# A row softmax: the first store is issued behind five instead of fourteen exponentials of the second tile

## The chip, the core and the metric

The kernel runs on one core of a Trainium2 chip. The engines that matter are VectorE (DVE), ScalarE (ACT), the sequencer SP that issues the loads, and the core's 16 DMA engines. The metric is the device time of one execution in microseconds, as the median of several runs.

## The reference

The input is 16 x 1024 x 512 float32 (33.55 MB), and the output has the same size. Every row of 512 gets a softmax at temperature 0.5:

```python
x_scaled = x / 0.5
x_max = np.max(x_scaled, axis=-1, keepdims=True)
exp_x = np.exp(x_scaled - x_max)
return exp_x / np.sum(exp_x, axis=-1, keepdims=True)
```

## The kernel before

The 16384 rows are cut into 8 tiles (c = 0 to 7). A tile has 128 partitions with 16 rows each, 4 MB, and a row's 512 elements lie one after another in its partition. Six buffers hold tiles; tiles 6 and 7 take the buffers of tiles 0 and 1, so their loads wait until the stores of those have landed. Everything is computed in place.

Tile 0 is loaded in two parts (4 rows and 12 rows of each partition), the others whole. All loads go through SP's queue (L66). All stores go through ACT's queue (L120), one for each tile, so ACT issues them in its own stream of instructions.

The work is cut into 11 blocks. Tile 0 has three (blocks 0, 1 and 2 with 4, 4 and 8 rows), tiles 1 to 6 are one block each (blocks 3 to 8), and tile 7 has two of 8 rows (blocks 9 and 10). A block goes through these steps:

- `shift` (L68): VectorE finds the negative maximum of each row (L74) and doubles it (L78): the bias. The load is issued here too, if the tile has none yet.
- `exponentials` (L80): ACT takes exp(2x + bias) row by row, one instruction for 512 elements of every partition, and sums as it goes (L86).
- `scale_vector` (L96): VectorE takes the reciprocals of the sums (L101) and multiplies the first rows, seven eighths of the block (L103).
- `scale_scalar` (L107): ACT multiplies the remaining rows, one for a block of 8 and two for a block of 16 (L112).
- `store` (L116): behind the tile's last block, the whole tile is written out.

The schedule is written by hand: each engine runs its instructions in the order of the program, and waits only where data or a buffer is missing. In step i of the loop ACT gets the exponentials of block i + 1, then the scaling of block i's last rows, then the store; VectorE gets the scaling of block i, then the maximum of block i + 2. `rows` (L127) cuts a block's exponentials into those ahead of the scaling and the store of the block before and those behind them. Only block 3, all of tile 1, is cut; the store beside it is that of tile 0, the first of the kernel.

Of the kernel before, what the change touches and what calls it, by code (L numbers as in the profile page):

```python
# [1 line left out]

# [4 lines left out]


@with_exitstack
def kernel(  # L10
    ctx: ExitStack,
    tc: tile.TileContext,
    x: bass.AP,
    out: bass.AP,
):
    nc = tc.nc
    fp32 = mybir.dt.float32
    P = nc.NUM_PARTITIONS
    AX = mybir.AxisListType.X
    EXP = mybir.ActivationFunctionType.Exp  # L20
    COPY = mybir.ActivationFunctionType.Copy
    MAX = mybir.AluOpType.max

    D = x.shape[-1]
    xf = x.flatten_outer_dims()
    of = out.flatten_outer_dims()
    N = xf.shape[0]

    G = 16
    C = N // (P * G)
    assert C * P * G == N
    xr = xf.rearrange("(c p g) d -> c p g d", p=P, g=G)
    outr = of.rearrange("(c p g) d -> c p g d", p=P, g=G)
    WHOLE = [(0, G)]
    LOADS = [[(0, 4), (4, G)]] + [WHOLE] * 7
    BLOCKS = [[(0, 4), (4, 8), (8, G)]] + [WHOLE] * 6 + [[(0, 8), (8, G)]]
    STORES = [WHOLE] * 8  # L40
    BMAX = 16
    BUFS = 6

    data = ctx.enter_context(tc.tile_pool(name="data", bufs=BUFS))
    stats = ctx.enter_context(tc.tile_pool(name="stats", bufs=6))

    ctx.enter_context(tc.manual_schedule())


    warm = stats.tile([P, 1], fp32, name="warm", bufs=1)  # L50
    nc.vector.memset(warm, 0.0)  # L51
    nc.scalar.activation(out=warm, in_=warm, func=EXP)  # L52

    chunks = {}
    blocks = [(c, lo, hi) for c in range(C) for lo, hi in BLOCKS[c]]
    n = len(blocks)
    biases, sums, recips = {}, {}, {}

    def load(c):
        if c < BUFS:  # L60
            chunks[c] = data.tile([P, G, D], fp32, name="xt")
        else:
            chunks[c] = chunks[c - BUFS]
        xt = chunks[c]
        for lo, hi in LOADS[c]:
            nc.sync.dma_start(out=xt[:, lo:hi, :], in_=xr[c][:, lo:hi, :])  # L66

    def shift(i):  # L68
        c, lo, hi = blocks[i]
        if c not in chunks:  # L70
            load(c)
        b = hi - lo
        negmax = stats.tile([P, BMAX], fp32, name="negmax")
        nc.vector.tensor_reduce(  # L74
            negmax[:, 0:b], chunks[c][:, lo:hi, :], axis=AX, op=MAX, negate=True
        )
        biases[i] = stats.tile([P, BMAX], fp32, name="bias")
        nc.vector.tensor_scalar_mul(biases[i][:, 0:b], negmax[:, 0:b], 2.0)  # L78

    def exponentials(i, rows):  # L80
        c, lo, hi = blocks[i]
        if i not in sums:
            sums[i] = stats.tile([P, BMAX], fp32, name="sums")
        for g in rows:
            row = chunks[c][:, lo + g, :]
            nc.scalar.activation(  # L86
                out=row,
                in_=row,
                func=EXP,
                bias=biases[i][:, g : g + 1],  # L90
                scale=2.0,
                accum_out=sums[i][:, g : g + 1],
            )


    def scale_vector(i):  # L96
        c, lo, hi = blocks[i]
        b = hi - lo
        k = b - b // 8
        recips[i] = stats.tile([P, BMAX], fp32, name="recip")  # L100
        nc.vector.reciprocal(recips[i][:, 0:b], sums[i][:, 0:b])  # L101
        rows = chunks[c][:, lo : lo + k, :]
        nc.vector.tensor_mul(  # L103
            rows, rows, recips[i][:, 0:k].unsqueeze(2).broadcast_to((P, k, D))
        )

    def scale_scalar(i):  # L107
        c, lo, hi = blocks[i]
        b = hi - lo
        for g in range(b - b // 8, b):  # L110
            row = chunks[c][:, lo + g, :]
            nc.scalar.activation(  # L112
                out=row, in_=row, func=COPY, scale=recips[i][:, g : g + 1]
            )

    def store(i):  # L116
        c, _, end = blocks[i]
        for lo, hi in STORES[c]:
            if hi == end:
                nc.scalar.dma_start(  # L120
                    out=outr[c][:, lo:hi, :], in_=chunks[c][:, lo:hi, :]
                )

    shift(0)
    shift(1)

    def rows(i):  # L127
        c, lo, hi = blocks[i]
        cut = hi - lo - (2 if c == 1 else 0)
        return range(cut), range(cut, hi - lo)  # L130

    exponentials(0, rows(0)[0])
    for i in range(n):
        if i + 1 < n:
            exponentials(i + 1, rows(i + 1)[0])
        scale_vector(i)
        scale_scalar(i)
        if i + 2 < n:
            shift(i + 2)
        store(i)  # L140
        if i + 1 < n:
            exponentials(i + 1, rows(i + 1)[1])


# [1 line left out]
_INS = ['x']  # L146
_OUTS = [((16, 1024, 512), 'float32')]


# [23 lines left out]
```

## Time and profile before

| what | us |
|---|---|
| median of 5 runs (162.05 to 162.61) | 162.33 |
| the profiled execution | 162.41 |
| its span, first to last instruction | 160.6 |
| VectorE busy | 134.6 |
| ACT busy | 102.2 |
| a maximum over 128x8192 (L74) | 8.68 |
| a scaling of 14 rows, 128x7168 (L103) | 7.62 |
| an exponential of one row (L86) | 0.71 |
| first store issued | 44.11 |
| last store issued | 147.50 |

Times inside an execution count from the span's start. In the profile's lines a group is named by line, engine, operation and what it writes and reads, `out<-in`; `xt` is a tile, `negmax`, `bias`, `sums` and `recip` are the small vectors of a block. `q1` and `q10` are the queues that the DMA engines serve, loads and stores. `ACTq` and `SPq` are instructions of the sequencers that issue DMAs; a DMA's issue takes under a microsecond, and its data moves later. "To landing" counts from the issue to the moment at which the whole transfer is announced.

### The profile page before, as it was taken

Reading aid. Unit: us, or ns where it says so; the run is one execution under the profiler, and the core shown is the slowest. Engines: PE = TensorE matmul, PEld = TensorE weight load, DVE = VectorE, ACT = ScalarE, POOL = GpSimd, SP = SyncE. Lnnn points to the kernel's source line nnn. Section 1 sums busy time; section 2 is a strip of 40 time slices with the busy share of each in tenths; the row PEclk is TensorE's granted clock in tenths of the full one; section 3 lists DMA queues with packets and bytes.
Section 4 is the critical chain, followed back from the end, with each engine's and each line's share of the span. In section 5 each row is a group of like instructions: output and inputs, shape, how many; then the busy total and the mean of one; then the engine's idle time right before and its main releaser. Section 6 shows DMA issues by size and latency. Waiting matters only on the chain.

```text
span 160.6 us, 402 instructions
## 1 busy us (share of the span) xinstructions
DVE 134.6 (84%) x45; ACT 102.2 (64%) x273; POOL 0.2 (0%) x4
## 2 busy tenths in 40 slices
DVE  0607999999999999999999999999999999957000
ACT  3071549069989963998199909990999890790000
POOL 0000000000000000000000000000000000000000
DMA  5999999999999999999999999999999999999993
GB/s 182 471 408 490 408 400 498 408 392 475 433 375 392 416 408 481 416 392 490 424 392 490 424 392 475 432 392 449 465 392 432 481 392 408 490 408 408 490 408 139
DMA packets 2450, 67.13 MB, mean 418 GB/s; under 512 B 272, under 2 KB 272, under 8 KB 272
## 3 DMA queue, kind: packets, MB, share of 16 engines
q1 hardware_dynamic: 1296, 33.56, 49.3%
q10 hardware_dynamic: 1152, 33.55, 48.4%
q14 instruction: 2, 0.02, 0.0%
HBM read 33.55 MB, written 33.55 MB: 418 GB/s over the span
## 4 chain that ended last, share of the span: by engine, by line
DVE 80%; DMA 7%; ACT 4%; issue 0%; SPq 0%
DVE negmax L74 42%; DVE xt L103 36%; DMA xt<-in_x_dram 7%; ACT xt L86 4%; DVE bias L78 1%; DVE recip L101 1%; SPq L66 0%
## 5 line engine op out<-in xcount | busy, mean ns | idle before, releaser
L86 ACT ACTIVATE xt<-xt,bias 128x512 f32<-128x512 f32 x128 | 90.4, 707 | 41.5 <-DVE bias L78 40.6
L74 DVE TENSOR_REDUCE negmax<-xt 128x16 f32<-128x8192 f32 (+2 forms) x11 | 69.9, 6353 | 9.5 <-DMA xt<-in_x_dram 9.5
L103 DVE TENSOR_TENSOR xt<-xt,recip 128x7168 f32<-128x7168 f32 (+2 forms) x11 | 62.0, 5637 | 0.4
L86 ACT ACTIVATION_READ_ACCUMULATOR xt<-xt,bias 128x1 f32 x128 | 23.8, 186 | 0.0
L112 ACT ACTIVATE xt<-xt,recip 128x512 f32<-128x512 f32 x15 | 9.9, 706 | 0.0
L101 DVE RECIPROCAL recip<-sums 128x16 f32<-128x16 f32 (+2 forms) x11 | 2.4, 219 | 1.8 <-ACT xt L86 1.8
L78 DVE TENSOR_SCALAR bias<-negmax 128x16 f32<-128x16 f32 (+2 forms) x11 | 1.9, 173 | 0.4
L52 ACT ACT_TABLE_LOAD x1 | 1.3, 1283 | 0.7 <-PEq L157 0.7
L51 DVE MEMSET warm<- 128x1 f32 x1 | 0.1, 59 | 0.8 <-PEq L157 0.8
L52 ACT ACTIVATE warm<-warm 128x1 f32<-128x1 f32 x1 | 0.2, 203 | 0.0
L157 POOL MEMSET const-bfloat16-1.0<- 128x1 bf16 x1 | 0.1, 101 | 0.0
L157 POOL MEMSET const-uint8-127<- 128x1 uint8 x1 | 0.1, 101 | 0.0
L157 POOL MEMSET const-float32-0.0<- 128x1 f32 x1 | 0.1, 98 | 0.2 <-issue 0.2
L157 POOL MEMSET const-float32-1.0<- 128x1 f32 x1 | 0.1, 98 | 0.0
## 6 DMA issues: line engine op xcount, KB each, us to landing
out_dram<-xt ACTq DMA_DIRECT2D x8, 4096.0 KB, 23.1
xt<-in_x_dram SPq DMA_DIRECT2D x7, 4096.0 KB, 30.1
xt<-in_x_dram SPq DMA_DIRECT2D x1, 3072.0 KB, 11.7
xt<-in_x_dram SPq DMA_DIRECT2D x1, 1024.0 KB, 4.8
```

The costliest lines, as they stand in the source:

```text
L51: nc.vector.memset(warm, 0.0)
L52: nc.scalar.activation(out=warm, in_=warm, func=EXP)
L74: nc.vector.tensor_reduce(negmax[:, 0:b], chunks[c][:, lo:hi, :], axis=AX, op=MAX, negate=True)
L78: nc.vector.tensor_scalar_mul(biases[i][:, 0:b], negmax[:, 0:b], 2.0)
L86: nc.scalar.activation(out=row, in_=row, func=EXP, bias=biases[i][:, g : g + 1], scale=2.0, accum_out=sums[i][:, g : g + 1],)
L101: nc.vector.reciprocal(recips[i][:, 0:b], sums[i][:, 0:b])
L103: nc.vector.tensor_mul(rows, rows, recips[i][:, 0:k].unsqueeze(2).broadcast_to((P, k, D)))
L112: nc.scalar.activation(out=row, in_=row, func=COPY, scale=recips[i][:, g : g + 1])
L157: nc = _bacc.Bacc("TRN2", target_bir_lowering=False, num_devices=1)
```

## The change

Block 3 is cut behind its fifth exponential instead of its fourteenth. ACT runs five exponentials of tile 1, scales the last row of tile 0, issues tile 0's store, and then runs the other eleven exponentials. Before it ran fourteen, scaled, stored, and ran two. Nothing else moves, on ACT or on any other engine.

```diff
     def rows(i):
         c, lo, hi = blocks[i]
-        cut = hi - lo - (2 if c == 1 else 0)
+        cut = 5 if c == 1 else hi - lo
         return range(cut), range(cut, hi - lo)
```

## The prediction

> **What bounds the kernel now.** I read the page's shares first, then the chain of work that ended last, then the DMA rows and queues.
>
> ```profile
> span 160.6 us, 402 instructions
> DVE 134.6 (84%) x45; ACT 102.2 (64%) x273; POOL 0.2 (0%) x4
> DMA  5999999999999999999999999999999999999993
> q1 hardware_dynamic: 1296, 33.56, 49.3%
> q10 hardware_dynamic: 1152, 33.55, 48.4%
> DVE 80%; DMA 7%; ACT 4%; issue 0%; SPq 0%
> ```
>
> Two resources are full. VectorE is named by the chain, but it stops at 147.4 us, 13.2 us before the end. The DMA engines are busy in every slice from the second to the last but one: q1 (loads) and q10 (stores) take 97.7% of the span, 156.9 us. The busy-time table of three stretches says what they move (columns: stretch, its length, DVE, ACT and POOL busy with counts, clock, DMA share, GB/s):
>
> ```profile
> 1.70:41.00 39.30, 30.43 (x15) 19.62 (x55) 0.00 (x0) 1.00 1.01 428
> 49.00:113.00 64.00, 63.73 (x17) 47.97 (x131) 0.00 (x0) 1.00 1.00 434
> 116.00:159.00 43.00, 29.46 (x11) 23.37 (x62) 0.00 (x0) 1.00 0.98 424
> ```
>
> Loads alone, loads beside stores, and stores alone run at one rate. So a store that comes earlier does not make the engines faster or slower; it takes turns from the loads. The size of a turn: q10's 1152 packets are 8 x 128 data packets of 32 KB and 8 x 16 tiny ones that announce the end, so 48.4% x 16 x 160.6 / 1024 = 1.21 us for a data packet on its engine; a 4 MB tile is 8 on each of 16 engines, 9.7 us alone.
>
> How turns are shared is read from the transfers' landings, each asked for by the stretch of its issue. Loads of tiles 1 and 2 (issued 1.62 and 2.09) land after 20.9 and 30.1 us, at 22.5 and 32.2: 9.7 apart, alone. Tiles 5, 6 and 7 land at 76.9, 96.2 and 116.3 (issued 3.82, 68.41, 87.79; 73.1, 27.8 and 28.5 later): 19.3 and 20.1 apart, beside stores. Loads and stores alternate one to one, and a load beside a store takes twice as long.
>
> The last load decides what follows. These are the landing times in the DMA answers for issues of 68 to 69 and of 87.5 to 88 us, the first store's, and the last store's:
>
> ```profile
> xt<-in_x_dram SPq DMA_DIRECT2D x1, 4096.0 KB, 27.8
> xt<-in_x_dram SPq DMA_DIRECT2D x1, 4096.0 KB, 28.5
> out_dram<-xt ACTq DMA_DIRECT2D x1, 4096.0 KB, 24.2
> out_dram<-xt ACTq DMA_DIRECT2D x1, 4096.0 KB, 12.3
> ```
>
> And these, from the timeline, are the instructions that they meet:
>
> ```profile
> 33.60 3.89 DVE L103 TENSOR_TENSOR xt<-xt,recip 128x3584 f32<-128x3584 f32 x1
> 37.03 0.71 ACT L86 ACTIVATE xt<-xt,bias 128x512 f32<-128x512 f32 x1
> 43.38 0.70 ACT L112 ACTIVATE xt<-xt,recip 128x512 f32<-128x512 f32 x1
> 44.11 0.38 ACTq L120 DMA_DIRECT2D out_dram<-xt  x1
> ...
> 103.88 8.68 DVE L74 TENSOR_REDUCE negmax<-xt 128x16 f32<-128x8192 f32 x1
> ...
> 120.50 4.41 DVE L74 TENSOR_REDUCE negmax<-xt 128x8 f32<-128x4096 f32 x1
> ...
> 147.50 0.34 ACTq L120 DMA_DIRECT2D out_dram<-xt  x1
> ```
>
> Tile 7 lands at 116.3 and VectorE asks for it at 120.50: a slack of 4.2 us, the number on which this change turns. Tile 6 lands at 96.2 and is asked for at 103.88, a slack of 7.7; tile 5 at 76.9 for 87.26, 10.4.
>
> **The change, part by part.** Nothing is added or removed. On ACT, nine of block 3's exponentials go from before the last-row scaling and the first store to behind them; the order on VectorE and SP is the same.
>
> *ACT and the moved issue.* The exponentials step by 0.705 us, so the sixth started at 37.03; there the last-row scaling now runs, to 37.74. It needs the reciprocal of 33.37, long there. The store also waits for VectorE's scaling of seven rows, which ends at 33.60 + 3.89 = 37.49. That is 0.25 us before ACT arrives, so the wait costs nothing; if VectorE were later by more, eleven instead of two exponentials of block 3 would stand behind the waiting store, and VectorE's reciprocal of their sums at 46.20 behind those. Today the last sum is ready at 45.87 + 0.19 = 46.06, 0.14 us ahead. The move leaves that: 16 exponentials, one scaling and one issue (a 0.45 us gap) in another order. The store goes out at 37.77 instead of 44.11, 6.34 us earlier. Cost on the path: 0, at most some tenths.
>
> *The loads.* Each store packet that comes earlier sits between load packets. 6.34 us of earlier start are 6.34 / 1.21 = 5.2 packets, so 5 or 6 on each engine, and all later loads land 5 x 1.21 = 6.1 us later (6 packets: 7.3). This holds only if the store queue never runs dry, which would give turns back. It does not: the first store would take from about 42.4 (issue + the 4.6 us between issue and first packet that the packet records show today) to about 61.8, and the second is issued at 58.97, the next ones at 75.59, 92.21 and 108.83, each before the one ahead is through at 19.4 us apiece (81, 100.6, 120). SP's queue is fed too: load 6 is let go when store 0 has landed, at about 62, and load 5 runs until about 82.
>
> *Who feels it.* Tile 5: 76.9 + 6.1 = 83.0, wanted at 87.26. Tile 6: 102.3, wanted at 103.88, still in time by 1.6. Tile 7: 116.3 + 6.1 = 122.4, wanted at 120.50: VectorE stands for 1.9 us. Here is the one uncertain size. The packet records put the ends of load 7 at 113.5 to 114.0 us on fifteen engines and at 115.85 on one, which lags by 1.87 us, or 1.5 packets. A lag of one packet only would give 1.25 us; no lag, 116.3 - 1.87 + 6.1 = 120.5 and a wait of nothing; a sixth packet, 3.1. Between 1.25 and 1.9 I take 1.55, since one engine out of sixteen is enough and the packets' order at the first store's entry makes one fall behind easily.
>
> *From VectorE to the end.* Behind the late reduce of L74 everything is serial: scaling of tile 6 (7.62), the second half's maximum (4.41), its scaling, eight exponentials on ACT, the last scaling, the last store. The one gap, 1.79 us before the reciprocal at 143.29, is spent waiting for ACT's exponentials, which hang on the same chain. So the last store goes out at 147.50 + 1.55 = 149.05. Meanwhile the engines will have done all other transfers at 148.5 to 149.7, as today, since they are full until then and tile 6's store (issued at 133.02 + 1.9 at most) is still ahead of its turn. What today's backlog costs the last store is small: it lands after 12.3 us, and on free engines 9.7 us plus what a small load shows beyond its bytes: 1 MB in 4.8 us, less 1.05 MB / 428 GB/s = 2.45, 2.35; together 12.05. So 0.25 us of the delay is absorbed. The sum: +1.55 - 0.25 = **+1.3 us**. The ends: 0 (no wait) and 3.1 - 0.25 = 2.9.
>
> The Trainium skill would price the last store differently: "DMA: Bandwidth & Descriptors", section "Anatomy of one DMA — SWDGE (gpsimd) path", fits 2.0 us plus bytes over 436 GB/s, 11.6 us for 4.19 MB, as an estimate. By that the backlog absorbs 0.7 us and the sum would be +0.85; the fit is for another issuing path, and the 4.8 us row is of this kernel.
>
> The profiled execution has 162.41 us, 1.8 more than its span; the median of five is 162.33. 162.33 + 1.3 = **163.6 us**.
>
> **The rivals.**
> - *No engine lags, and the load is just in time (same, 162.3).* By the working above the wait then is 0.0 to 0.2 us, which the 0.25 absorbs. For it: the lag of one engine grew out of small irregularities that need not come again. Against it: sixteen engines must all keep step.
> - *Faster, by the backlog.* If the earlier store meant less work left for the engines at 147.5, the last store would run on free ones: 147.50 + 12.05 instead of 12.3, -0.25, and with the 1.87 us lag of one engine gone as well at most some 0.9 us less: 161.5. It decides where tile 7 lands before 120.50 and the engines lose less when the first store enters: the stretch 41.0 to 48.7 us moves 400 GB/s against 428, a loss of 7.7 x 0.065 = 0.5 us. Against it: the engines are full, and order does not change the sum.
> - *The first store takes hold sooner (slower still).* If its 4.6 us shrink to about 1, as for the first load, which the packet records show moving 1.0 us after its issue, loads lose more turns. The limit is store 1's issue at 58.97: it then starts at about 60 instead of 68.1, so no more than 8.1 us are lost. Tile 7 lands at 124.4, the wait is 3.9 us, the time 162.33 + 3.65 = 166.0.
> - *The store's wait blocks ACT.* VectorE would have to be over 0.25 us later than it is at 37.49; each further us would go through the sums to 46.20. Nothing ahead of it changes, so this stays at some tenths.
>
> **How the numbers follow.** A measurement can tell about 0.2%, 0.33 us, from no change. The slower case with a wait of 1 to 2.2 us: 0.57 (own range 162.8 to 164.3). Just in time, and the blocked ACT with it: 0.27. Sooner hold or a sixth packet: 0.10. Faster: 0.06. The first and third are slower but for a small part: slower 0.69, same 0.25, faster 0.06. The range of 8 in 10 reaches into the just-in-time case below (162.1) and to a sixth packet above (2.9 less the last few tenths: 164.9).
>
> **What would show it.** The first store issued near 37.8 us with no wait; loads of tiles 4 to 7 landing about 6 us later; an idle time of 1 to 2 us on VectorE before the first 128x4096 maximum of tile 7, ended by the DMA; the last store's issue later by as much. If tile 7 lands by 120.5, the load's step was wrong; if VectorE waits and the end does not move, the backlog's.

## The result, and the profile after

The changed kernel takes 162.69 us (median of 25 runs, 162.39 to 164.62 and one of 166.64) against 162.22 us for the kernel before (46 runs, 162.03 to 162.61). The ratio is 1.0035 with a 95% interval of 1.0025 to 1.0045. Ratios leave out executions that took over 1.5% longer than the fastest of their kernel, here the one of 166.64 us. It is slower, as forecast, but by 0.47 us by the medians and not by 1.3, and its times spread further. The profiled execution took 162.48 us, near the lower end; that of the kernel before took 162.41, above its median. So these two profiles are only 0.07 us apart, and most of the 0.47 us is not in them.

The page of the changed kernel, to set beside the lines of the prediction:

```profile
span 160.7 us, 402 instructions
DVE 134.7 (84%) x45; ACT 102.2 (64%) x273; POOL 0.2 (0%) x4
DMA  5999999999799999999999999999999999999994
q1 hardware_dynamic: 1296, 33.56, 49.4%
q10 hardware_dynamic: 1152, 33.55, 48.6%
q14 instruction: 2, 0.02, 0.0%
DMA 46%; DVE 34%; ACT 11%; issue 1%; SPq 0%
```

The engines compute for the same time. The chain of work that ended last has moved from VectorE (80% before) to the DMA (46%): somewhere an engine now waits for a transfer. And the two DMA queues take 98.0% of 160.7 us where they took 97.7% of 160.6: 157.5 instead of 156.9 us for the same bytes.

The timeline of the changed kernel, with the same instructions as in the prediction:

```profile
37.19 0.71 ACT L112 ACTIVATE xt<-xt,recip 128x512 f32<-128x512 f32 x1
37.93 0.37 ACTq L120 DMA_DIRECT2D out_dram<-xt  x1
...
104.04 8.68 DVE L74 TENSOR_REDUCE negmax<-xt 128x16 f32<-128x8192 f32 x1
...
121.24 4.42 DVE L74 TENSOR_REDUCE negmax<-xt 128x8 f32<-128x4096 f32 x1 [0.49 <-DMA xt<-in_x_dram]
...
148.23 0.34 ACTq L120 DMA_DIRECT2D out_dram<-xt  x1
```

The first store goes out at 37.93, with no wait, as forecast. VectorE does wait for tile 7: 0.49 us of idle time ahead of the maximum at 121.24. The last store goes out at 148.23 instead of 147.50, 0.73 us later; 0.16 us of that is a later start of the whole program's work (104.04 against 103.88), and 0.57 is the wait with what hangs on it.

The landings of the loads of tiles 6 and 7 (issued 62.73 and 82.62), of the first store and of the last one, each from the answer for the stretch of its issue:

```profile
xt<-in_x_dram SPq DMA_DIRECT2D x1, 4096.0 KB, 39.1
xt<-in_x_dram SPq DMA_DIRECT2D x1, 4096.0 KB, 38.6
out_dram<-xt ACTq DMA_DIRECT2D x1, 4096.0 KB, 24.7
out_dram<-xt ACTq DMA_DIRECT2D x1, 4096.0 KB, 11.6
```

Tile 6 lands at 101.8, tile 7 at 121.2. It landed at 116.3 before, so the load lost 4.9 us, four turns of 1.21, and not five. This is the landing on the slowest engine. By the packet records its last packet of this load stood behind 27 store packets in the kernel before, where the other fifteen engines had 26; in the changed kernel it stands behind 31, and the others behind 30 or 31. The last store lands 11.6 us after its issue, where it took 12.3: 0.7 us of its delay is made up at once. Its last data end at 159.50 us, against 159.42 before.

One relation holds in all twenty profiles of this study and orders what follows: **the device time is the end of the last store's data plus 2.95 to 3.04 us.** The end of the data is that of the slowest of 16 DMA engines. In the kernel before fifteen of them end at 158.3 to 158.8 and one at 159.42; in the changed one they end at 158.8 to 159.5. The middle engine ends 0.65 us later, the last one 0.08. The records name no engine: packets are put together to sixteen chains in which one begins as the one before ends, so single counts of engines can be off by one or two.

### The profile page after: what moved, and what is told of

It is laid out like the page before. It is cut to its first block, busy times and chain, and to the rows that moved or that the text cites. A ratio compares the mean times of both kernels' runs of the same rounds, so it can differ in the third digit from the quotient of the medians.

```text
span 160.7 us, 402 instructions
## 1 busy us (share of the span) xinstructions
DVE 134.7 (84%) x45; ACT 102.2 (64%) x273; POOL 0.2 (0%) x4
## 4 chain that ended last, share of the span: by engine, by line
DMA 46%; DVE 34%; ACT 11%; issue 1%; SPq 0%
DMA xt<-in_x_dram 31%; DVE negmax L74 20%; DMA out_dram<-xt 15%; DVE xt L103 12%; ACT xt L86 10%; ACT xt L112 1%; DVE bias L78 1%; DVE recip L101 0%; SPq L66 0%
```

## The experiments

Kernels named "before with" or "changed with" differ from that kernel by the lines shown. Ratios are to runs of the kernel before on the same chip, with the 95% interval.

### The changed kernel once more

> The changed kernel once more, unaltered, for a second profile of it. Theory A (VectorE waits for tile 7's load; the wait varies from execution to execution because it is set by the DMA engine that lags most): ratio 1.002 to 1.005 to the kernel before, VectorE's wait before the first half's maximum of tile 7 anywhere from 0 to 2 us, and the last store's issue later than 147.5 by that wait. Theory B (the added time is lost on the DMA engines, where the packets of the two queues meet differently, and VectorE's wait is beside the point): the same ratio, but data of the last store ends later by more or less than VectorE's wait explains.

Measured: 1.0027 (1.0014 to 1.0040). In its profile VectorE idles 0.88 us ahead of tile 7's first half, the last store goes out at 148.40, the data end at 159.66. The wait is 0.4 us longer than in the first profile, the end 0.16 us later. That fits both theories, and left the question open.

### Taking the wait, or its consequence, away

```diff
-    LOADS = [[(0, 4), (4, G)]] + [WHOLE] * 7
+    LOADS = [[(0, 4), (4, G)]] + [WHOLE] * 6 + [[(0, 8), (8, G)]]
```

> Changed kernel with tile 7 loaded in two halves of 2 MB, so that VectorE's first maximum of tile 7 needs only the first half. The first half should land some 9 us before 121.2, at about 112, and be wanted at 120.5. Theory A: no wait before that maximum, the last store issued at 147.5 to 147.7, time equal to the kernel before: ratio 0.999 to 1.001. Theory B: the order of the two queues' packets on the engines is as in the changed kernel, so the ratio stays 1.003 or more.

> Kernel before with tile 7 loaded in two halves and nothing else changed: the control for the two halves. Theory C: the engines are in step as before except for one or two, ratio 0.999 to 1.001, so that the halves by themselves cost nothing. If the halves cost something (a further end marker, an engine out of step), it shows here as 1.001 to 1.003.

Measured: the changed kernel with the halved load 1.0024 (1.0015 to 1.0034), without any wait and with the last store issued at 147.58. But the kernel before with the halved load has 1.0044 (1.0031 to 1.0057): the halves cost something by themselves (in its profile fifteen engines end by 158.51, and one at 160.13). So the pair decides nothing; without the control it would have looked like a proof.

```diff
-    STORES = [WHOLE] * 8
+    STORES = [WHOLE] * 7 + [[(0, 8), (8, G)]]
```

> Changed kernel with tile 7 stored in two halves of 2 MB; the first half goes out behind its last scaled row at about 144.5, the second at about 148.2. VectorE's wait for tile 7 stays (0.5 to 2 us). Theory A with the step that the wait costs time only because the engines run out of stores before the last one is issued: the first half now fills them, so the wait is hidden and the time equals the kernel before, ratio 0.998 to 1.001. If the wait costs time otherwise than through the engines' running out, the ratio stays 1.003.

> Kernel before with tile 7 stored in two halves: the control for the halves. In the kernel before the engines have no idle time ahead of the last store, so there is nothing to fill: ratio 0.999 to 1.001. If halves of a store cost by themselves, as halves of the last load did (1.0044), 1.001 to 1.004.

Measured: changed with the halved store 1.0030 (1.0015 to 1.0044); before with it 1.0003 (0.9995 to 1.0012). This control is clean. VectorE still idles 0.55 us, the engines now have work until the last issue at 148.21, and nothing is gained. The added time is not the engines' running out of stores, so the prediction's last step is in doubt.

### The price of the wait alone

```diff
+    pad = stats.tile([P, 520], fp32, name="pad", bufs=1)     # 1360 in the longer one
+    nc.vector.memset(pad, 0.0)
+    low = stats.tile([P, 1], fp32, name="low", bufs=1)
...
         negmax = stats.tile([P, BMAX], fp32, name="negmax")
+        if i == 9:
+            nc.vector.tensor_reduce(low, pad, axis=AX, op=MAX)
```

> Kernel before with a maximum over 520 idle elements put ahead of VectorE's first maximum of tile 7: it delays everything behind it by about 0.57 us, as the wait of the changed kernel's profile does, and moves no transfer but the last store, which goes out at about 148.05. Prices the wait alone. In the kernel before fifteen engines end at 158.2 to 158.8 and one at 159.4, so the delay has to use up that lag first. Theory D: idle time of some engines ahead of the last store, mean end later by 0.1 to 0.3 us, ratio 0.9995 to 1.0015. By the prediction's 0.25 us of absorption: 1.002.

> As the one before with 1360 elements, about 1.46 us: the wait that the prediction forecast. Last store issued at about 148.95. Theory D: all engines but the last stand idle by 0.5 to 1.2 us, mean end at about 159.4, the lagging one at 159.9 to 160.1, ratio 1.003 to 1.005. By the prediction's absorption of 0.25 us: +1.2 us, 1.0075.

The timeline of the longer one shows what is put in:

```profile
120.47 1.56 DVE L79 TENSOR_REDUCE low<-pad 128x1 f32<-128x1360 f32 x1
121.95 4.41 DVE L80 TENSOR_REDUCE negmax<-xt 128x8 f32<-128x4096 f32 x1
```

Measured: with 520 elements VectorE's maximum of tile 7 starts 0.60 us later than it could have (120.96 instead of 120.36), the last store goes out at 147.94, and the ratio is 0.9999 (0.9990 to 1.0008). With 1360 elements the delay is 1.48 us (121.95 instead of 120.47), the store goes out at 148.93, 1.43 us later than in the kernel before, and the ratio is 1.0023 (1.0013 to 1.0034), 0.37 us. So in the kernel before a wait of the size found in the first profile is **free**, and the one forecast would cost 0.4 us, not 1.3. Some 1.1 us are covered, where the prediction had 0.25. The reason shows in the last store's landing, 11.6 us with the shorter delay and, with the longer one,

```profile
out_dram<-xt ACTq DMA_DIRECT2D x1, 4096.0 KB, 11.1
```

that is 11.1 us, against 12.3 in the kernel before. On idle engines its first packet moves 0.84 us after the issue and all 16 start nearly together; in the kernel before it stands behind an engine that ends its earlier work at 149.73, 1.2 us after the first one is free.

### Packets that take longer: how early the first store goes out

Now the packet records. In the kernel before nearly every 32 KB data packet takes 1.213 us, but for a few around the first store's entry. In the changed kernel, from 64 to 112 us, where loads and stores alternate, the mean is 1.226 us. That this can cost time without any wait is shown by the kernels with other numbers of exponentials ahead of the first store:

```diff
-        cut = hi - lo - (2 if c == 1 else 0)
+        cut = 9 if c == 1 else hi - lo           # and 8, and 7
```

> First store behind nine exponentials of tile 1, at about 40.6 us, between the kernel before (44.1) and the changed one (37.8). Tile 0's store should end on the engines near 64.5, and tile 1's, issued at 59.0, is to hand at 62.5, so the engines keep in step; three store packets come earlier, tile 7 lands at about 120.0 at most and is wanted at 120.5. Theories A and C: no wait, ratio 0.999 to 1.001. A cost in proportion to how early the first store is: 1.0015 to 1.002.

> Eight exponentials: between nine (0.9997) and seven (1.0098). First store at about 39.8 us. Three or four store packets come earlier than in the kernel before, so tile 7 lands at 120 to 121.2 and the wait is 0 to 0.7 us. Theory E: a wait of that size is covered by the engine that ends last, ratio 0.999 to 1.001 if the packets stay at 1.213 us between 60 and 118 us, and 1.002 to 1.01 if they get longer as with seven.

> First store behind seven exponentials, issued at about 39.2 us: between nine (no cost) and five. Four store packets come earlier than in the kernel before, so tile 7 lands 4 x 1.21 = 4.9 us later, at about 121.1, and VectorE waits about 0.5 us. Tile 0's store ends at 62 to 63.2 and tile 1's is to hand at 62.4 to 62.6, so some engines may run dry for a turn. Theory D: ratio 1.0005 to 1.003, the more the more engines are out of step. A cost from five exponentials alone (the first store entering together with the boundary of tiles 3 and 4): 1.000.

> Seven exponentials once more, for a profile of an undisturbed execution: the first one's profile was of a disturbed execution, while its undisturbed ones gave 1.0098. Theory E (the wait for tile 7 costs only beyond about 1.3 us, and here it is beyond): no turn is given back at the second store, some engines' packets take longer, tile 7 lands at 122.5 to 124 and VectorE waits 2 to 3.5 us; the last store is issued at 149.5 to 151 and ends 0.85 + 9.8 us later; ratio 1.007 to 1.012. If the wait is below 1.3 us, the added time is longer packets on an engine that lags.

| exponentials ahead | first store | ratio | interval |
|---|---|---|---|
| 14 (before) | 44.11 | 1 | |
| 9 | 40.53 | 0.9997 | 0.9989 to 1.0006 |
| 8 | 39.78 | 1.0068 | 1.0044 to 1.0092 |
| 7 | 38.97, 39.18 | 1.0098, and 1.0196 the second time | 1.0079 to 1.0117, 1.0167 to 1.0224 |
| 5 (changed) | 37.93 | 1.0035 | 1.0025 to 1.0045 |

The cost is not in proportion to the shift: nothing at nine, more at eight and seven than at five. With seven the times spread widely, from 163.47 to 169.09 us in the first six runs and from 164.71 to 166.98 in the second six. Of the kernel with eight, these are the waits of VectorE for loads (waiter, releaser: total us, times, longest), the maximum of tile 7's first half, and the last store:

```profile
DVE negmax L74 <- DMA xt<-in_x_dram: 9.4, 2, 4.8
```

```profile
120.40 4.41 DVE L74 TENSOR_REDUCE negmax<-xt 128x8 f32<-128x4096 f32 x1
...
147.39 0.34 ACTq L120 DMA_DIRECT2D out_dram<-xt  x1
```

VectorE waits twice, for tile 0 at the start, as before, and not for tile 7; the last store is as early as ever. Still this execution took 162.75 us (the fastest of its six; the median is 163.46). Its loads and stores are slower where they alternate. The busy-time table from 64 to 116 us, with DMA share and GB/s last, of nine and of eight exponentials:

```profile
64.00:116.00 52.00, 51.79 (x13) 39.98 (x109) 0.00 (x0) 1.00 1.00 433
```

```profile
64.00:116.00 52.00, 51.79 (x13) 39.98 (x109) 0.00 (x0) 1.00 1.00 424
```

Both are full (share 1.00), but 433 and 424 GB/s are moved. The packets have 1.214 us on average in the one and 1.232 in the other, and the last data end at 159.19 and 159.78. The three engines that end last carry 1.1 to 1.4 us of such excess. So in that execution, the fastest of this kernel, the longer packets are the whole loss against nine: 0.59 us, with no wait.

With seven, longer packets and a wait meet. The timeline of the second run:

```profile
105.76 8.69 DVE L74 TENSOR_REDUCE negmax<-xt 128x16 f32<-128x8192 f32 x1 [1.80 <-DMA xt<-in_x_dram]
125.66 4.42 DVE L74 TENSOR_REDUCE negmax<-xt 128x8 f32<-128x4096 f32 x1 [3.19 <-DMA xt<-in_x_dram]
...
152.65 0.34 ACTq L120 DMA_DIRECT2D out_dram<-xt  x1
```

One DMA engine has store packets of 1.3 to 1.8 us from 64 us on, in sum some 5.5 us more than at 1.213, and ends the load of tile 7 at 124.06; thirteen others end it by 118.0, the remaining two by 119.7. A tile has landed when its slowest engine is through, so VectorE waits 1.8 us for tile 6 and 3.2 for tile 7. Now the wait is far beyond the 1.1 us that are covered: most of the engines stand idle for 3.8 to 4.9 us ahead of the last store, and the data end at 164.00.

### What makes the engines differ: the second store

In the packet records of the changed kernel tile 0's store and the load of tile 4 end together at 61.3 us on most engines. Tile 1's store was issued at 59.13, but its first packet moves at 62.69, so on about ten of the engines two load packets follow each other there: one turn is given back to the loads. Some engines had taken the first store a turn earlier, meet this point at another place, and from then on read while others write. This was tried from both sides, first by issuing the second store earlier in the changed kernel:

```diff
-        cut = 5 if c == 1 else hi - lo
+        cut = {1: 5, 2: 11}.get(c, hi - lo)
```

> Changed kernel with tile 1's store also issued earlier: behind 11 of block 4's 16 exponentials, at about 55.7 instead of 59.1 us. In the changed kernel that store's first packet moves 3.5 us after its issue, at 62.7, and the store queue stands empty for one turn behind tile 0's store (two load packets follow each other at 61.3 and 62.5 us). Theory A with the step that this empty turn gave 1.2 us back to the loads: now it is not given back, tile 7 lands about 1.2 us later, VectorE waits about 1.2 us longer, ratio 1.009 to 1.012 to the kernel before. If the empty turn is of no account: ratio 1.003 to 1.005 as in the changed kernel.

> Changed kernel with tile 1's store issued at 55.7 us, and tile 7 loaded in two halves: the engines keep in step and VectorE does not wait. Theory C with a small rest of theory A (the ratio of 1.0014 with the early second store alone is VectorE's wait of 0.7 us): ratio 1.000, between 0.999 and 1.001. If the earlier first store costs something by itself: 1.0015 or more.

> Changed kernel with both mends: tile 1's store issued at 55.7 us (keeps the engines in step) and tile 7 stored in two halves (fills the engines while VectorE's late work ends). Theory D: the added time has two parts that cover each other, the longer packets of engines out of step (0.46 us on average over the engines in the changed kernel) and the engines' idle time before the last store (0.55 us more than before with the early second store alone). With both taken away the mean end of the engines is back at that of the kernel before (158.5), ratio 0.998 to 1.001, although VectorE still waits 0.5 to 1 us for tile 7. If the early first store costs something else: 1.0015 or more.

Measured: 1.0014 (1.0002 to 1.0026) with the early second store alone. The forecast of 1.009 to 1.012 was wrong; by the medians the kernel is faster than the changed one (the intervals overlap). In its profile nearly all engines keep in step and the mean packet is 1.215 us; VectorE idles 0.51 us, and the last data end at 159.32. No engine has two load packets in a row at 61 us, and yet VectorE starts on tile 7 at 121.31, as early as in the changed kernel (121.24): that the given-back turn brought the landing forward is not shown. With the halved load it is 1.0038 (1.0022 to 1.0053), with the halved store 1.0025 (1.0016 to 1.0035), both above what was expected. Their packets are at 1.214 us, so longer packets from 64 to 112 us are not what is lost there. In the latter, tile 7's first maximum waits longer:

```profile
122.82 4.42 DVE L74 TENSOR_REDUCE negmax<-xt 128x8 f32<-128x4096 f32 x1 [2.42 <-DMA xt<-in_x_dram]
```

It waits 2.4 us, 1.9 more than with the early second store alone. Here the first store came in a turn earlier on most engines (behind 40 load packets instead of 41), though nothing in the edits asks for it. In both profiles one engine ends last: at 159.92 with the halved store and 160.01 with the halved load, 1.2 and 0.9 us behind the middle one. Ahead of the first store's first packet, at 38.5 to 40.6 us, single packets lasted over 2.1 us. The theory does not explain this part of the loss.

Then by issuing the second store later in the kernel before, so that it comes to hand as the engines reach for it (the rows' scaling is moved along to hold it back; in the first attempt only the store was moved):

```diff
+            if i == 5 and g == 1:
+                for _ in range(2):      # 3 in the third attempt
+                    nc.scalar.activation(out=warm, in_=warm, func=COPY)
+                scale_scalar(3)
+                store(3)
...      # and both are taken out of their old places
```

> Kernel before with one thing moved: tile 1's store is issued behind the third exponential of tile 3, at about 65.1 instead of 59.0 us. Tile 0's store ends on the engines at 66.9 to 68.0 us; with some 3.5 us from issue to first packet, tile 1's store now comes to hand at about 68.6, as in the changed kernel just behind the end of the store before it. Theory C (the engines fall out of step there: some get one load packet more than others, from then on some read while others write, and such packets take a few per cent longer): engines out of step rise from about 2 to 4 to 7 of 16 between 68 and 114 us, the packets' excess grows by 0.3 to 1 us of span, ratio 1.002 to 1.005, without any wait of VectorE for tile 7, which lands at about 115 to 116.5. Theory A (only VectorE's wait costs): ratio 0.999 to 1.001.

> Kernel before with tile 1's last two rows scaled, and its store issued, behind the first exponential of tile 3 and two tiny instructions on ACT: at about 65.4 us instead of 59.0. The store then comes to hand at about 68.9 us, just as the engines reach for it (68.7 to 69.2), some in time and some a turn too late. Theory D: engines out of step rise from about 2 to 4 or more of 16 behind 69 us, the packets' excess grows by 0.2 to 0.8 us of span, and the ratio is 1.001 to 1.004, without any wait of VectorE for tile 7. If all engines fall on the same side, they stay in step and the ratio is 1.000. Theory A (VectorE's wait alone costs): ratio 0.999 to 1.001 with the engines out of step.

> The late second store once more, 0.2 us later (three tiny instructions ahead of it instead of two): issued at about 65.46, to hand at about 68.9, within the 68.6 to 69.2 us in which the engines reach for it. Two times before all engines had fallen on one side. Theory D: now some miss a turn, engines out of step rise to 4 or more of 16 from 69 to 114 us, the packets' excess grows by 0.2 to 0.8 us, ratio 1.001 to 1.004, with no wait for tile 7. If the packets stay at 1.213 us although engines are out of step, being out of step is not what makes them longer, and the ratio is 1.000.

Measured: 1.0004 (0.9995 to 1.0012), 1.0005 (0.9994 to 1.0015) and 1.0000 (0.9991 to 1.0008), with the store issued at 62.90, 65.26 and 65.52. None of them put many engines out of step: in the first the store was issued 2.2 us earlier than meant, as nothing held it back, and came early enough for all; in the second one engine missed the turn; in the last all missed it together (first packet 69.23). These three show only that a late second store, and a missed turn, cost nothing as long as nearly all engines do the same.

Put together, this is worked out from the packet records of the profiled executions. "Minority" is the mean number of engines that read while more write, or the other way round, from 64 to 112 us; "packet" is the mean time of a 32 KB packet there.

```
kernel                             minority   packet us   last issue   last data
before                                  1.8       1.214       147.50      159.42
before, 9 exponentials                  1.6       1.214       147.44      159.19
before, second store 65.52              1.4       1.214       147.44      159.34
before, delay 520                       1.6       1.214       147.94      159.20
before, delay 1360                      1.7       1.214       148.93      159.68
changed, second store early             2.2       1.215       148.30      159.32
  the same, halved load                 3.4       1.214       147.28      160.01
  the same, halved store                2.3       1.214       149.83      159.92
changed                                 5.8       1.226       148.23      159.50
changed, again                          3.9       1.219       148.40      159.66
changed, halved store                   5.6       1.229       148.21      159.61
changed, halved load                    5.3       1.233       147.58      160.21
before, 8 exponentials                  5.9       1.232       147.39      159.78
before, 7 exponentials, again           3.0       1.234       152.65      164.00
```

Of the profiles listed, all with longer packets have three or more engines out of step, and all but one of the others fewer. The exception (3.4 engines and 1.214 us) says that being out of step is not enough. What else it takes stays open. (The first profile with seven exponentials, of 169.09 us, has 3.3 engines and 1.249 us.)

The table's means say little of the engine that ends last, and that one alone sets the time. In the kernel before and in both profiles of the changed one it is at work without a break from its first packet to its last. So no wait of VectorE holds it up, and its end is the sum of its packets. This is what its 32 KB packets take beyond 1.213 us each:

| kernel | ahead of 60 us | 64 to 112 us | last data |
|---|---|---|---|
| before | 1.15 | 0.25 | 159.42 |
| changed | 1.29 | 0.36 | 159.50 |
| changed, again | 1.36 | 0.37 | 159.66 |
| second store early, halved store | 1.63 | 0.37 | 159.92 |
| second store early, halved load | 1.81 | 0.37 | 160.01 |

The engines with long packets between 64 and 112 us in the changed kernel (up to 0.95 us of excess) are others, which end earlier. So in these profiles being out of step adds some 0.1 us to the end, and the packets around the first store's entry at least as much; in the first of them this engine also began its work 0.17 us earlier.

### A store queue used early

The first load's 1 MB was issued on ACT's queue, ahead of the work there, with tile 7 stored in halves, to learn whether the loss at the first store's entry (0.93 us on average over the engines, 44 to 48 us) belongs to the first use of that queue.

```diff
-            nc.sync.dma_start(out=xt[:, lo:hi, :], in_=xr[c][:, lo:hi, :])
+            eng = nc.scalar if (c, lo) == (0, 0) else nc.sync
+            eng.dma_start(out=xt[:, lo:hi, :], in_=xr[c][:, lo:hi, :])
...      # this load moves ahead of ACT's other work; STORES as above
```

> Kernel before with the first 1 MB load issued on ACT's queue, ahead of everything else there, and tile 7 stored in halves. In the kernel before the first store's coming makes two packets on every engine longer, 0.93 us of span in all, right behind the first use of that queue. If this belongs to the first use of a queue, it moves to the start, where it meets the same cost of the other queue: the engines gain 0.5 to 0.9 us, ratio 0.994 to 0.998. If it belongs to the first writes to memory, it stays at 45 to 49 us: ratio 0.999 to 1.002. The first load shares turns with the second and lands some 2.4 us later, which VectorE's 4.7 us of idle time behind it take up.

Measured: 1.0118 (1.0100 to 1.0137). The loss stays with the first store (0.73 us on average at 48 to 52 us), so it is not the queue's first use. The rest is a mistake of the edit: packets of 8 and 24 KB took turns one for one, so the small load landed at about 13.4 us together with the larger one instead of 2.4 us late, and all of VectorE's work began later.

## Why the prediction was right and wrong

- **The moved issue and ACT's order: right.** Forecast 37.77, found 37.93 with the whole program 0.16 later; no wait; the sums in time.
- **"All later loads land 5 x 1.21 = 6.1 us later": wrong by one turn on the engine that counts.** Most engines had five load packets fewer before the first store (41 instead of 46), as forecast. But the engine that ends tile 7's load last already stood one turn behind the others in the kernel before (27 store packets ahead of its last load packet, against 26) and went to 31: four turns, and a landing at 121.2, not 122.4. **"This holds only if the store queue never runs dry ... It does not": wrong too.** The second store needed 3.56 us from issue to first packet beside loads, a time that the sum left out, and about ten engines gave a turn back. What that turn is worth in the landing is not shown.
- **"VectorE stands for 1.9 us ... I take 1.55": 0.57 in the first profile and 0.96 in the second** (the last store's delay without the shift of the whole program; VectorE's idle time is 0.49 and 0.88). The 1.9 us less the turn of 1.2 and the later start of 0.16 leave 0.54, near the 0.57 found.
- **"So 0.25 us of the delay is absorbed": the term of the sum that was most mis-sized.** Measured, a delay of 0.6 us costs nothing and one of 1.48 us costs 0.37: some 1.1 us are absorbed. By this alone the forecast wait would have cost 0.4 us and the one found nothing. The 12.05 us that I put together for the last store on free engines, from a 1 MB load's landing, are 11.1. The estimate of 11.6 from the Trainium skill's "DMA: Bandwidth & Descriptors" was nearer, though also too high. I also looked at how far the last store was behind its issue, and not at how far the slowest engine was behind the others, which I had read in the packet records for the load and not for the end.
- **"A store that comes earlier does not make the engines faster or slower; it takes turns from the loads": wrong, a term put at nothing.** The three rates of the stretches hid it, since they are all of the kernel before, in which the engines keep in step. In the changed kernel's first profile the packets take 0.46 us more on the average engine, and 0.25 us more on the engine that ends last. That longer packets cost time without a wait is shown by eight exponentials; that filling the engines' idle time does not help the changed kernel, by the halved store. That being out of step is part of the loss is made likely, and not more, by the early second store: 1.0014 with the engines in step and the wait as before. How the 0.47 us of the medians divides is not known, since the profiles hold only 0.07 and 0.24 us of it.
- So the sign was right by luck: it was forecast for a wait that is real but costs nothing in both profiles, and the time they lose is in packets that take longer, which the prediction did not have.
- **The rivals.** "Just in time" was near: the wait is there but covered. "The first store takes hold sooner" and "the store's wait blocks ACT" did not come (entry 4.2 us after the issue, 4.6 before). "Faster, by the backlog" had its 0.25 us from the wrong price.

Not settled: what makes packets longer, once engines are out of step and at the first store's entry, which also costs the two kernels with the early second store and a halved transfer their time; and how much of the changed kernel's median, 0.2 us above its first profile, is longer waits in other executions.

## What to carry to other kernels

Where the DMA engines are full, the end is that of the slowest of sixteen; ask of a late last transfer how far that engine is behind the others before pricing the delay, and put the delay in by itself (an idle instruction) to measure its price. A slack of 4 us on a load, which no wait shows, leaves room for one slow engine (with seven exponentials one was 6 us behind most others); the kernels here that spent it spread further even where the median hardly moved, 162.39 to 164.62 us against 162.03 to 162.61. Why they spread is not shown. And run the control of an experiment's own edit: halving a load cost more than the effect that it was to isolate.

## What the runs showed of the hardware

- A queue's turn is spent even by the tiny packet that announces a transfer's end: it takes 9 ns, and then the other queue has two data packets of 1.21 us in a row. Where the ends of a load and a store meet, both turns cancel. The round that the Trainium skill describes in "DMA: Bandwidth & Descriptors", section "Queues, rings and completion order", one packet from each queue in turn, is what the records show; that an end marker counts as such a packet shows only there.
- The page's `q14 instruction` line is two packets of 8 KB, 0.31 us each, at 37.6 and 97.1 us in the kernel before, both on one DMA engine. It is the engine that ends last, 0.94 us behind the middle one.
- Between the first store's issue and its first packet, or just behind, one or two packets on every engine take mostly 1.3 to 2.1 us instead of 1.21 (about 0.9 us of span in most runs, and up to 1.7), also where its queue has carried a load before.
- From issue to first packet a store took 3.4 to 4.6 us beside loads and 0.84 to 0.86 us on engines that had nothing else.
